# Three quarters of a conditioning product moved from VectorE to ScalarE and GpSimd

## The chip, the core and the metric

The kernel runs on one core of a Trainium2 chip. Its engines work side by side, each through its own queue in order: TensorE (PE; its weight loads are PEld) multiplies matrices, VectorE (DVE), ScalarE (ACT) and GpSimd (POOL) do elementwise work, and SyncE (SP) issues most of the DMAs that bring the weights. The metric is the device time of one execution in microseconds (us); smaller is better.

## What is computed

Two layers of a decoder trunk act on 256 tokens of 2048 features, in float32. Layer 0 has a mixer made of a gated part and a convolution, layer 1 has attention; each layer ends with a channel MLP of 8192 hidden channels. Before each of the four parts the input is normalised, scaled and shifted, and behind it the result is gated. Shift, scale and gate come from a conditioning vector `c`:

```python
c_act = jax.nn.silu(c)
for l in range(DEPTH):
    mod = c_act @ ada_w[l] + ada_b[l]
    shift1, scale1, gate1, shift2, scale2, gate2 = jnp.split(mod, 6, axis=-1)
    h = _modulate(_rms(x, norm1_g[l]), shift1, scale1)
    ...
    x = x + gate1[:, None, :] * mix
    h = _modulate(_rms(x, norm2_g[l]), shift2, scale2)
    x = x + gate2[:, None, :] * (jnp.square(jax.nn.relu(h @ mlp_w1[l])) @ mlp_w2[l])
```

`ada_w[l]` is 2048 by 12288, so the conditioning is a product of one vector with a large matrix: much weight traffic, little arithmetic for each weight. The change concerns `shift2` and `scale2` of layer 0.

## The kernel before

**Weights.** Each product of the tokens with a weight matrix runs over tiles of 512 by 512 weights (1 MiB). `wraw` (L111) issues the tile's DMA from SyncE into one of four buffers of the pool `raw`. `wtile` (L124) splits the tile into a high and a low part: ScalarE converts the tile (`wh`, L94) and VectorE subtracts that from it (`wl`, L95, both operands in SBUF). There are three buffers for `wh` and two for `wl`. A tile then feeds 24 matmuls of 128x512 (three for each of 4 feature blocks and 2 halves of the tokens, L183 to L185, or L210 to L212 in the first products of the MLP).

**Side work.** Behind each weight tile `side_work` (L135) takes steps from `ada_queue`, so many to a tile as the step's rate says. A conditioning step loads 1 MiB of `ada_w` into a `raw` buffer, too, multiplies it by values of `c` and adds it up. `ada_until` (L332) runs the steps that are left at once when their result is needed.

**The columns.** `ada_quarters` (L246) computes two columns side by side, here shift and scale of the MLP in layer 0 (columns 3 and 4). It goes by quarters of 512 features: eight steps to a quarter (four groups of inputs for each of two columns), four products to a step. A sum lies in `accq`, [128, 512] for each column, in two sets that alternate by quarter. In three quarters of the four, VectorE does product and sum in one instruction (L269), and the first product of a sum by L267. In the first quarter (`aided=1`) ScalarE makes the product (L263) into one of four places of the tile `side`, and GpSimd adds it to the sum (L265). When a sum is complete, `ada_finish_col` transposes it on TensorE (L107), reduces it on VectorE (L221) and adds the bias (L223).

**Where this lies.** `even` (L474) builds 32 such steps (L507). The eight of the first quarter are mixed with the steps of the mixer's gate row (`ada_row`, L278, which also uses ScalarE, GpSimd and `side`). The other 24 follow beside the tiles of the mixer's output product (`ab_w_out`, 16 tiles): four of them at rate `RA` (2.5 to a tile), twenty at `R1` (0.8 to a tile). The MLP then begins at L419. Its loop (L430 to L437) forces a quarter's steps (`ada_until`, L432), normalises and modulates 512 features (`norm_quarter`, L373: `xn` L354 on VectorE, transposes, `full` L380 on ScalarE, `h_h` L382 and `h_l` L383 on VectorE), and runs the three first products over the quarter before (`gemm_quarter`, L189, three tiles of `mlp_w1`).

**Other names that come up.** The convolution's taps (L542) run on VectorE and read PSUM. `layer_norm` (L603) normalises the convolution's output on VectorE and ScalarE. The gate row is spread over the partitions by two matmuls for each 512 features (L311, L312), which ScalarE copies out (L313). `residual` (L401) adds to `x` (L411, L412), and `sum_squares` (L337) squares it. `x_rstd` (L342) makes the inverse root of the norm in a chain of tiny VectorE instructions (L345 to L349, with L72 to L90). Temporary tiles of 512 columns (`junk`, `xn`, `full`, `rt` and others) share six buffers of the pool `tmp` under the tag `t512`.

**Order.** The place of an instruction in its engine's queue is set by the framework when the program is built: it follows the order of the program's text, but puts an instruction ahead where its own time model says that it is ready first. Buffers and waits come from it as well. On an engine, an instruction that waits holds up all that stand behind it.

Of the kernel before, what the change touches and what calls it, by code (L numbers as in the profile page):

```python
# [42 lines left out]
class Trunk:  # L43
    def __init__(self, ctx, tc, t):
        self.tc, self.nc, self.t = tc, tc.nc, t
        pool = lambda n, b, **k: ctx.enter_context(tc.tile_pool(name=n, bufs=b, **k))
        self.const = pool("const", 1)
        self.raw = pool("raw", 4)
        self.wh = pool("wh", 3)
        self.wl = pool("wl", 2)  # L50
        self.act = pool("act", 4)
        self.tmp = pool("tmp", 6)
        self.ext = pool("ext", 1)
        self.small = pool("small", 3)
        self.mm = pool("mm", 4, space=bass.MemoryType.PSUM)
        self.tr = pool("tr", 2, space=bass.MemoryType.PSUM)
        self.ms = pool("ms", 2, space=bass.MemoryType.PSUM)
        self.ada_queue = []
        self.ada_credit = 0.0
        self.conv_queue = []  # L60
        self.hold = False
        self.first = 0  # tiles still to be split by GpSimd
        self.conv_rate = 10
        self.conv_y = {}
        self.quarters = {}

# [1 line left out]
    def rsqrt(self, out, v):  # L68
        """out = v ** -0.5 for v > 0: a first guess from the bits, a third-order step, a Newton step."""
        nc = self.nc  # L70
        n = v.shape[-1]
        nc.vector.tensor_scalar(out.bitcast(I32), v.bitcast(I32), -0.5, float(0x5F3759DF), op0=ALU.mult, op1=ALU.add)  # L72
        pool, tag = (self.small, "nr") if n <= 16 else (self.tmp, "t512")
        a = pool.tile([P, 2, n], F32, tag=tag, name="nr")
        w, b = a[:, 0, :], a[:, 1, :]

        def square_times(f):
            if n == 1:
                nc.vector.scalar_tensor_tensor(w, out, f, out, op0=ALU.mult, op1=ALU.mult)
            else:  # L80
                nc.vector.tensor_tensor(w, out, out, op=ALU.mult)
                nc.vector.tensor_tensor(w, w, f, op=ALU.mult)

        # out <- 8/3 of its third-order step, then Newton with the 8/3 taken out again
        nc.vector.tensor_scalar(b, v, -0.5 * (3 / 8) ** 3, None, op0=ALU.mult)
        square_times(v)
        nc.vector.scalar_tensor_tensor(w, w, -10 / 3, w, op0=ALU.add, op1=ALU.mult)
        nc.vector.scalar_tensor_tensor(out, w, 5.0, out, op0=ALU.add, op1=ALU.mult)
        square_times(b)
        nc.vector.scalar_tensor_tensor(out, w, 1.5 * 3 / 8, out, op0=ALU.add, op1=ALU.mult)  # L90

    def split(self, src, hi, lo, engine=None):
        """src = hi + lo, both with the 12 significant bits that one pass of the array takes."""
        self.nc.scalar.copy(hi, src)  # L94
        (engine or self.nc.vector).tensor_tensor(lo, src, hi.bitcast(F32), op=ALU.subtract)  # L95
# [6 lines left out]
    def transpose4(self, srcs):  # L102
        """Up to four [128, n] blocks -> one PSUM bank, transposed side by side."""
        ps = self.tr.tile([P, 512], F32, tag="tr", name="trp")
        for i, s in enumerate(srcs):
            w = s.shape[-1]
            self.nc.tensor.transpose(ps[:w, i * P : i * P + s.shape[0]], s, self.ident[: s.shape[0], : s.shape[0]])  # L107
        return ps

# [14 lines left out]
    def wtile(self, w, k0, nk, n0, nw):  # L124
# [3 lines left out]
        # VectorE is busy with the norm when a phase's first tiles come: GpSimd splits those  # L128
# [6 lines left out]
    def side_work(self, size=1.0):  # L135
        """Work that is spread beside the weight tiles: conditioning and the convolution."""
# [10 lines left out]
    def gemm32(self, ps, x, w, g, n0):  # L147
        """ps += x[:, 512 features of group g] @ w[those, n0:n0+512], whole float32 passes."""
# [12 lines left out]
    def gemm(self, x, xk0, w, k0, nkb, n0, nw, skew=False):  # L161
        """[256, nw] = x[:, K] @ w[K, n0:n0+nw], as two PSUM tiles of 128 tokens; with skew the
        first half of the tokens is complete well before the second."""
# [25 lines left out]
    def gemm_quarter(self, units, x, q, paired):  # L189
        """512 features of x into each of units = (psum, w, n0, nw); with paired, the first half of  # L190
        the tokens of two units goes before their second half."""
# [23 lines left out]
    # mod = silu(c) @ ada_w + ada_b, one 1 MiB piece of ada_w to a step  # L215
    def ada_finish_col(self, out, layer, j, q, acc):
        """Feature-major column sums of acc [128, 512], plus the bias."""
# [7 lines left out]
    def ada_col(self, layer, j):  # L225
        """self.mod[layer, j] = [128, 16], feature-major."""
# [19 lines left out]
    def ada_quarters(self, layer, j0, side=None, aided=0):  # L246
        """Columns j0 and j0 + 1 side by side, complete for 512 features after every eight steps.
        The first aided quarters go by ScalarE and GpSimd, with room for products in side."""
# [3 lines left out]
        def step(q, g, i):  # L252
# [6 lines left out]
            for k in range(4):  # L259
                c = self.cT[:, 4 * g + k : 4 * g + k + 1]  # L260
                if q < aided:
                    prod = acc if g + k == 0 else side[:, D + k * 512 : D + (k + 1) * 512]
# [15 lines left out]
    def ada_row(self, layer, j, side=None):  # L278
        """self.mod[layer, j] = [128, 2048], the same in every partition. With side = [128, 4096],
        the products go to ScalarE and the sums to GpSimd."""  # L280
# [37 lines left out]
    def at_end(self, last):  # L318
        """Before the last product of a stage: no more work beside it."""
# [3 lines left out]
    def ada_more(self, rate, *lists):  # L323
        """Steps to be worked off beside the coming weight tiles, rate steps to a tile."""
# [26 lines left out]
    def norm_t(self, h, q, r):  # L351
        """Four blocks of (x * r).T in PSUM."""
# [4 lines left out]
    def norm_start(self, layer, which):  # L357
        """A function that gives 512 features' (shift, gain) columns: modulate(rms(x) * g) = x * rstd * gain + shift."""
# [14 lines left out]
    def norm_quarter(self, quarter, q, pair):  # L373
        """512 features of h.T, as (hi, lo)."""
# [10 lines left out]
    def norm_mod(self, layer, which):  # L385
        """h.T (hi, lo) of modulate(rms(x) * g, shift, scale)."""
# [6 lines left out]
    def gated(self, src, gate, h, c):  # L393
        """x[:, chunk] += gate * src, for one half"""
# [6 lines left out]
    def residual(self, ps, gate, c, last, part=None):  # L401
        """x[:, chunk] += gate * (ps + part)"""
# [16 lines left out]
    def mlp(self, layer, last):  # L419
# [8 lines left out]
        # the first three chunks take the features as the modulation completes them  # L428
# [9 lines left out]
        # sums over the blocks of hidden channels  # L438
# [35 lines left out]
    def even(self, layer):  # L474
# [14 lines left out]
        # mixer B  # L489
# [17 lines left out]
        g1, q34 = self.ada_row(layer, 2, side), self.ada_quarters(layer, 3, side, 1)  # L507
# [16 lines left out]
        def glu(j, pa, pg):  # L524
# [8 lines left out]
            def tap(b, k):  # L533
                # read from PSUM, which leaves GpSimd its port to SBUF
# [9 lines left out]
            # two sums side by side, so that no tap waits on the one before  # L544
# [11 lines left out]
        # mixer A  # L556
# [46 lines left out]
        def layer_norm():  # L603
            """LayerNorm over channels (the partition axis), swish."""
# [24 lines left out]
        # mixer A's rows of the first three chunks, then mixer B's  # L629
# [18 lines left out]
    def rms_columns(self, srcs):  # L648
        """1 / rms along the free axis of each of some [128, n], as the columns of one tile."""
# [18 lines left out]
    def low_rank(self, src, r, gcol, pair, k0, h):  # L668
        """One half's [128, 512], scaled by its rms r and by g, transposed and split."""
# [11 lines left out]
    def rope(self, out, src, tab, n):  # L681
        """Rotary pairs of [128, n, 64]; tab = [128, 128]: (C1 | C2), (-S2 | S1)."""
# [8 lines left out]
    def odd(self, layer):  # L691
# [12 lines left out]
        # columns 512:1088 = c_kv and the rotary key, as pieces of 320 and 256 columns  # L704
# [21 lines left out]
        # two heads at a time: keys, values and queries, then scores, then the output, a step apart  # L726
# [10 lines left out]
        def squares(c, s, src):  # L737
            """Sums of squares of [P, half, head, n], as row s of three."""
# [20 lines left out]
        def normalized(c):  # L759
# [8 lines left out]
            # rotary pairs of both halves  # L768
# [16 lines left out]
        def scores(c):  # L785
# [3 lines left out]
            for i in range(2):  # L789
                rows = slice(i * ROPE, (i + 1) * ROPE)  # L790
                sc = self.ms.tile([P, 512], F32, tag="ms", name="sc")
                # query block 1 sees 256 keys, query block 0 the first 128
# [18 lines left out]
        def weights_t(ss):  # L811
            out = []
            for s in ss:
                # transposed: keys 0..127 for query blocks 0 and 1, keys 128..255 for block 1
# [45 lines left out]
    def setup(self):  # L860
# [15 lines left out]
        # 128-long rows that become per-partition columns  # L876
# [43 lines left out]
    def setup_even(self):  # L920
        nc, t, c = self.nc, self.t, self.const
        # conv taps: rows (tap, block) -> columns
# [12 lines left out]
        # spatial weights, lower triangle, transposed  # L935
# [10 lines left out]
    def setup_odd(self, room):  # L946
        """Mask and rotary tables, with room [128, 768] for the raw ones."""
        nc, t = self.nc, self.t
        # causal mask: query block 1 on 256 keys, then query block 0 on 128
# [9 lines left out]
        # rotary tables of both halves with the head gains  # L959
# [39 lines left out]
def rope_table():  # L999
    """cos | sin of the rotary angles, [256, 64]: by shape alone."""  # L1000
# [23 lines left out]
```

## Time and profile before

| | |
|---|---|
| timed runs | 2189.75 us median of 3 (2189.74 to 2189.92) |
| profiled execution, first to last instruction (span) | 2185.9 us |
| around the span, against the median | 3.85 us |
| instructions | 23655 |
| weight bytes read from HBM | 564.06 MB, 259 GB/s over the span |
| GpSimd busy over the span | 146.7 us (7%) |

The profile records one execution; it gives its span, and no time of its own around it. PE, DVE, ACT and POOL in its views are the engines; "busy" is the time in which an engine had an instruction running. A row of the view of groups gives line, engine, operation, output <- inputs, the shape, how many there were, and then busy time, mean duration in ns, and the idle time in front of them with the work that ended it. A timeline row gives start, duration and so on for instructions merged where they are alike and follow one another. PEclk is the share of TensorE's clock that was granted. Where a row says "A <- B", A waited for B.

### The profile page before, as it was taken

How to read it: one execution, taken by the hardware profiler on the slowest of the kernel's cores; microseconds unless marked ns; L12 is line 12 of the kernel's file. 1: busy time of each engine (PE TensorE's matmuls, PEld its weight loads, DVE VectorE, ACT ScalarE, POOL GpSimd, SP SyncE). 2: the span in 40 equal slices, each digit the busy share in tenths (PEclk: the TensorE clock that was granted, in tenths of full speed). 3: DMA queues.
4: the chain of work that ended last, by engine and by line, in shares of the span. 5: the costliest groups of instructions: out<-in, count | busy, mean ns of one | idle time of the engine just before them, and what ended most of it. 6: DMA issues, size and time to landing. Idle time of an engine off the chain costs nothing.

```text
span 2185.9 us, 23655 instructions
## 1 busy us (share of the span) xinstructions
PE 2090.9 (96%) x9138; PEld 1635.7 (75%) x9138; DVE 1564.9 (72%) x1763; ACT 932.3 (43%) x1184; POOL 146.7 (7%) x95
## 2 busy tenths in 40 slices
PE   2889999899999999999998999989999999999999
PEld 1444458678888888888888787868888888888887
DVE  6849999888777878787767878766656545554555
ACT  2135435444444334333436776444434433433432
POOL 0038710000000000000001000010000000000000
PEclk9999999899999999999999999989999999999999
DMA  9999968899898899989755646647778556556653
GB/s 350 384 346 330 332 242 295 275 317 339 315 337 315 329 326 319 339 304 334 270 174 174 211 158 214 229 154 250 256 271 264 178 192 189 189 192 192 189 191 122
DMA packets 238620, 567.70 MB, mean 260 GB/s; under 512 B 9150, under 2 KB 17784, under 8 KB 221864
## 3 DMA queue, kind: packets, MB, share of 16 engines
q1 hardware_dynamic: 236288, 562.60, 74.3%
q10 hardware_dynamic: 1564, 2.28, 0.3%
q8 instruction: 72, 1.18, 0.2%
q0 software_dynamic: 656, 1.31, 0.2%
q14 instruction: 40, 0.33, 0.0%
HBM read 564.06 MB, written 2.10 MB: 259 GB/s over the span
## 4 chain that ended last, share of the span: by engine, by line
PE 85%; DVE 9%; DMA 5%; ACT 1%; issue 1%; SPq 0%; ACTq 0%; DVEq 0%
PE mm L183 23%; PE mm L184 23%; PE mm L185 23%; PE mm L153 4%; DMA raw<-in_ada_w 4%; PE trp L107 3%; DVE accq L269 2%; DVE cvsq L542 1%; DVE wl L95 1%; PE mm L210 1%; PE mm L211 1%; PE mm L212 1%; PE sc L797 1%; PE sc L796 1%; DMA raw<-in_mlp_w 1%
## 5 line engine op out<-in xcount | busy, mean ns | idle before, releaser
L95 DVE TENSOR_TENSOR wl<-raw,wh 128x2048 fp32r<-128x2048 f32 (+2 forms) x312 | 704.7, 2259 | 424.0 <-PE mm L184 317.9
L94 ACT CAST wh<-raw 128x2048 fp32r<-128x2048 f32 (+3 forms) x316 | 596.6, 1888 | 774.1 <-PE mm L185 515.2
L183 PE MATMUL mm<-wh,f_h 128*128 128x512 f32 x1024 | 399.6, 390 | 0.0
L185 PE MATMUL mm<-wh,f_l 128*128 128x512 f32 x1024 | 399.3, 390 | 0.0
L184 PE MATMUL mm<-wl,f_h 128*128 128x512 f32 x1024 | 398.7, 389 | 0.0
L185 PE MATMUL mm<-wh,h_l 128*128 128x512 f32 (+2 forms) x928 | 358.2, 386 | 0.0
L183 PE MATMUL mm<-wh,h_h 128*128 128x512 f32 (+2 forms) x928 | 358.2, 386 | 0.0
L184 PE MATMUL mm<-wl,h_h 128*128 128x512 f32 (+2 forms) x928 | 357.0, 385 | 0.6 <-DVE wl L95 0.6
L185 PEld LDWEIGHTS mm<-wh,f_l 128*128 128x128 f32 x1024 | 192.2, 188 | 39.8
L184 PEld LDWEIGHTS mm<-wl,f_h 128*128 128x128 f32 x1024 | 192.3, 188 | 39.6
L183 PEld LDWEIGHTS mm<-wh,f_h 128*128 128x128 f32 x1024 | 192.3, 188 | 39.2
L184 PEld LDWEIGHTS mm<-wl,h_h 128*128 128x128 f32 x928 | 175.0, 189 | 34.0 <-DVE wl L95 1.1
L185 PEld LDWEIGHTS mm<-wh,h_l 128*128 128x128 f32 x928 | 174.9, 188 | 33.4
L183 PEld LDWEIGHTS mm<-wh,h_h 128*128 128x128 f32 x928 | 175.0, 189 | 32.7
L153 PE MATMUL mm<-raw,x 128*128 128x512 f32 x448 | 195.7, 596 | 1.0 <-ACT x L500 0.6
L269 DVE SCALAR_TENSOR_TENSOR accq<-raw,cT,accq 128x512 f32<-128x512 f32 x210 | 153.7, 749 | 16.6 <-DMA raw<-in_ada_w 13.3
L153 PEld LDWEIGHTS mm<-raw,x 128*128 128x128 f32 x448 | 84.6, 191 | 104.6 <-issue 98.5
L237 DVE SCALAR_TENSOR_TENSOR acc<-raw,cT,acc 128x2048 f32<-128x2048 f32 x60 | 140.8, 2346 | 9.7 <-DMA raw<-in_ada_w 9.7
L297 DVE SCALAR_TENSOR_TENSOR acc<-raw,cT,acc 128x2048 f32<-128x2048 f32 x48 | 112.7, 2347 | 4.4 <-DMA raw<-in_ada_w 4.4
L542 DVE SCALAR_TENSOR_TENSOR cvsq<-yp,convw,cvsq 128x256 f32<-128x256 f32 x240 | 96.0, 476 | 0.0
L303 POOL TENSOR_TENSOR side<-side 128x1024 f32<-128x1024 f32 x32 | 74.8, 2361 | 19.3 <-ACT side L302 19.3
L452 ACT ACTIVATE relu<-mm 128x512 f32<-128x512 f32 x60 | 35.8, 599 | 87.7 <-PE mm L185 81.5
(270 smaller groups left out, 2246.9 us busy)
## 6 DMA issues: line engine op xcount, KB each, us to landing
raw<-in_mlp_w SPq DMA_DIRECT2D x256, 1024.0 KB, 5.6
raw<-in_ada_w SPq DMA_DIRECT2D x192, 1024.0 KB, 5.4
raw<-in_ab_w_in SPq DMA_DIRECT2D x32, 1024.0 KB, 9.7
raw<-in_ab_w_out SPq DMA_DIRECT2D x16, 1024.0 KB, 8.3
raw<-in_mla_w_out SPq DMA_DIRECT2D x16, 1024.0 KB, 4.9
raw<-in_mla_w_ukv SPq DMA_DIRECT2D x8, 1024.0 KB
raw<-in_mla_w_uq SPq DMA_DIRECT2D x8, 768.0 KB, 4.8
raw<-in_mla_w_in SPq DMA_DIRECT2D x4, 1024.0 KB, 7.2
```

What stands on the lines that cost most here:

```text
L94: self.nc.scalar.copy(hi, src)
L95: (engine or self.nc.vector).tensor_tensor(lo, src, hi.bitcast(F32), op=ALU.subtract)
L107: self.nc.tensor.transpose(ps[:w, i * P : i * P + s.shape[0]], s, self.ident[: s.shape[0], : s.shape[0]])
L153: self.nc.tensor.matmul(ps[h], x[:, 4 * g + k, h * P : (h + 1) * P], raw[:, k, :], start=g + k == 0, stop=4 * g + k == KB - 1,)
L183: nc.tensor.matmul(o, a, hi[:, i, :nw], start=first, stop=False)
L184: nc.tensor.matmul(o, a, lo[:, i, :nw], start=False, stop=False)
L185: nc.tensor.matmul(o, b, hi[:, i, :nw], start=False, stop=last)
L237: nc.vector.scalar_tensor_tensor(acc, raw, self.cT[:, kb : kb + 1], acc, op0=ALU.mult, op1=ALU.add)
L269: self.last = nc.vector.scalar_tensor_tensor(acc, raw[:, k, :], c, acc, op0=ALU.mult, op1=ALU.add).ins
L297: nc.vector.scalar_tensor_tensor(acc, raw, c, acc, op0=ALU.mult, op1=ALU.add)
L303: nc.gpsimd.tensor_tensor(acc[:, sl], acc[:, sl], prod, op=ALU.add)
L542: nc.vector.scalar_tensor_tensor(o, y, wk, o, op0=ALU.mult, op1=ALU.add)
```

## The change

The function `ada_quarters` gets a further argument `late`. From the quarter `late[0]` on, a step's products go to ScalarE and its sums to GpSimd, as in the aided quarters. The product of such a quarter is put into a buffer of the tag `t512` and not into `side`. The call for the columns 3 and 4 of layer 0 passes `late=(1,)`, that is, the second, third and fourth quarter. The other call of `ada_quarters` (columns 0 and 1 of layer 0) passes nothing and stays as it is. The rest of the diff takes comments and doc strings out. Lines behind L261 move down by five.

```diff
-    def ada_quarters(self, layer, j0, side=None, aided=0):
+    def ada_quarters(self, layer, j0, side=None, aided=0, late=None):
...
-                if q < aided:
-                    prod = acc if g + k == 0 else side[:, D + k * 512 : D + (k + 1) * 512]
+                if q < aided or (late and q >= late[0]):
+                    if g + k == 0:
+                        prod = acc
+                    elif q < aided:
+                        prod = side[:, D + k * 512 : D + (k + 1) * 512]
+                    else:
+                        prod = self.tmp.tile([P, 512], F32, tag="t512", name="prod")
                     nc.scalar.activation(prod, raw[:, k, :], AF.Copy, scale=c)
                     if g + k:
                         nc.gpsimd.tensor_tensor(acc, acc, prod, op=ALU.add)
...
-        g1, q34 = self.ada_row(layer, 2, side), self.ada_quarters(layer, 3, side, 1)
+        g1, q34 = self.ada_row(layer, 2, side), self.ada_quarters(layer, 3, side, 1, (1,))
```

## The prediction

> **What bounds the kernel now.** I read the page first, then the view of windows over the stretch that the change touches, then who TensorE waited for in it, then VectorE's groups.
>
> ```profile
> span 2185.9 us, 23655 instructions
> PE 2090.9 (96%) x9138; PEld 1635.7 (75%) x9138; DVE 1564.9 (72%) x1763; ACT 932.3 (43%) x1184; POOL 146.7 (7%) x95
> ```
>
> Over the whole kernel TensorE is the bound: 96% busy. Time can be won only where it waits or runs at a low clock. The columns' last sums run on VectorE, where these two groups stand for 283 to 458 us:
>
> ```profile
> L269 DVE SCALAR_TENSOR_TENSOR accq<-raw,cT,accq 128x512 f32<-128x512 f32 x90 | 65.6, 747 | 0.6
> L267 DVE TENSOR_SCALAR accq<-raw,cT 128x512 f32<-128x512 f32 x6 | 2.8, 479 | 0.0
> ```
>
> That is 96 instructions, 24 steps of four: all that the change moves lies in this stretch of 175 us. Its windows (busy time of each engine, then PEclk, DMA share, GB/s):
>
> ```profile
> 283.00:294.00 11.00, 11.00 (x30) 5.00 (x29) 11.00 (x25) 1.90 (x1) 0.00 (x0) 1.00 0.30 109
> 294.00:330.00 36.00, 30.81 (x132) 23.51 (x131) 33.72 (x57) 13.50 (x16) 0.00 (x0) 0.86 0.67 233
> 330.00:411.00 81.00, 81.00 (x365) 66.55 (x363) 77.26 (x93) 37.27 (x37) 0.00 (x0) 1.00 0.91 316
> 411.00:458.00 47.00, 36.79 (x158) 29.86 (x158) 41.11 (x72) 20.21 (x34) 0.00 (x0) 0.85 0.77 260
> sum 175.00, PE 159.60 PEld 124.92 DVE 163.09 ACT 72.88 POOL 0.00; mean PE 39.90 PEld 31.23 DVE 40.77 ACT 18.22 POOL 0.00
> ```
>
> Here VectorE is the fuller engine (163.1 of 175 us), ScalarE has 102 us free, and GpSimd does nothing. TensorE loses time at two places, for these reasons:
>
> ```profile
> PE trp L107 <- DVE nr L87: 8.0, 1, 8.0
> PE gps L311 <- ACT gate L313: 4.4, 1, 4.4
> PE mm L210 <- DVE h_h L382: 2.3, 1, 2.3
> ```
>
> Together 14.7 us. SyncE, too, is held up by VectorE, which keeps the raw buffers:
>
> ```profile
> SPq L118 <- DVE accq L269: 66.0, 21, 10.9
> SPq L118 <- DVE wl L95: 47.2, 15, 6.7
> ```
>
> So the stretch is bound by VectorE's queue at its ends, and by TensorE from 330 to 411 us, where it never stops.
>
> **What the change removes.** 90 x 747 ns and 6 x 479 ns leave VectorE: 68.4 us of its 163.1 us by busy time.
>
> **What it adds.** 96 products on ScalarE and 90 sums on GpSimd. The same pair ran in the first quarter (min/median/max in ns):
>
> ```profile
> L263 ACT ACTIVATE side<-raw,cT x30: 705/712/722, 149.8 to 277.6; 128x512 f32<-128x512 f32 x30
> L265 POOL TENSOR_TENSOR accq<-accq,side x30: 1262/1272/1832, 152.1 to 281.2; 128x512 f32<-128x512 f32 x30
> ```
>
> ScalarE: 96 x 0.712 = 68.4 us, beside 72.9 us that it has: 141 of 175. By busy time that is covered by its free time; the price of its order is a rival below. GpSimd: 90 x 1.272 = 114.5 us, also under 175. If nothing else were shared, the change would fit. SyncE issues the same 24 DMAs of 1 MiB at the same places of its queue; only who frees their buffers changes. Transposes, reductions and bias adds of a finished column stay.
>
> **What GpSimd and VectorE share.** The trace shows them hold each other up. Before the stretch, VectorE did tiny instructions while GpSimd added:
>
> ```profile
> 245.38 0.16 DVE L72 TENSOR_SCALAR rv<-ssv 128x16 int32<-128x16 int32 x1
> 245.46 2.33 DVE L85 TENSOR_SCALAR nr<-ssv 128x16 f32<-128x16 f32 x1
> 247.71 0.47 DVE L542 SCALAR_TENSOR_TENSOR cvsq<-yp,convw,cvsq 128x256 f32<-128x256 f32 x1
> 248.10 2.00 DVE L81 TENSOR_TENSOR nr<-rv 128x16 f32<-128x16 f32 x1
> 245.37 4.70 POOL L303 TENSOR_TENSOR side<-side 128x1024 f32<-128x1024 f32 x2 [0.33 <-ACT side L302]
> ```
>
> L85 on 16 columns took 2.33 us: it ended where the first of the two additions ended. L81 took 2.00 us, to the end of the second. The convolution's tap between them, which reads PSUM, ran its 0.47 us beside the second addition. The other way round:
>
> ```profile
> 273.83 1.48 DVE L95 TENSOR_TENSOR gl<-side,gh 128x512 fp32r<-128x512 f32 x1
> 275.63 0.67 DVE L95 TENSOR_TENSOR gl<-side,gh 128x512 fp32r<-128x512 f32 x1
> 276.62 0.68 DVE L95 TENSOR_TENSOR gl<-side,gh 128x512 fp32r<-128x512 f32 x1
> 276.59 1.83 POOL L265 TENSOR_TENSOR accq<-accq,side 128x512 f32<-128x512 f32 x1 [1.83 <-ACT side L263]
> ```
>
> The first `gl` waited for an addition to end; during the third, GpSimd's sum took 1.83 instead of 1.27 us. So an instruction of VectorE that works from SBUF and an addition of GpSimd take turns, each for its whole length. What VectorE still has of this kind in the stretch:
>
> ```profile
> L95 DVE TENSOR_TENSOR wl<-raw,wh 128x2048 fp32r<-128x2048 f32 x22 | 50.3, 2287 | 3.6 <-PE mm L211 1.6 <-ACT wh L94 1.3 <-PE mm L184 0.3
> L412 DVE TENSOR_TENSOR x<-x,rt 128x512 f32<-128x512 f32 x8 | 5.5, 688 | 0.0
> L383 DVE TENSOR_TENSOR h_l<-full,h_h 128x512 fp32r<-128x512 f32 x6 | 4.1, 685 | 0.0
> L354 DVE TENSOR_SCALAR xn<-x,r 128x512 f32<-128x512 f32 x7 | 3.4, 481 | 0.0
> L382 DVE CAST h_h<-full 128x512 fp32r<-128x512 f32 x6 | 2.5, 423 | 3.5 <-ACT full L380 3.5
> L95 DVE TENSOR_TENSOR cat_l<-cvsq,cat_h 128x1024 fp32r<-128x1024 f32 x2 | 2.4, 1220 | 0.0
> L622 DVE TENSOR_TENSOR cvsq<-cvsq,rs 128x1024 f32<-128x1024 f32 x2 | 2.4, 1220 | 0.0
> L612 DVE TENSOR_TENSOR cvsq<-cvsq,mu 128x1024 f32<-128x1024 f32 x2 | 2.4, 1222 | 0.0
> L81 DVE TENSOR_TENSOR nr<-rs 128x256 f32<-128x256 f32 x2 | 0.8, 418 | 0.0
> L85 DVE TENSOR_SCALAR nr<-var 128x256 f32<-128x256 f32 x1 | 0.3, 288 | 0.0
> ```
>
> The first eight groups are 73.0 us; from L81 to L85 stand 19 small groups on SBUF (those two are the first and the last) with 8.0 us. Sum 81.0 us. The groups that read PSUM (taps, `rt`, L596, L221) aren't counted.
>
> **The sum.** Turns taken one after the other: 114.5 + 81.0 = 195.5 us in a stretch of 175, so 20.5 us too much. VectorE idled 175 - 163.1 = 11.9 us of it, mostly waiting for ScalarE and TensorE; I take it that this stays, since those waits are of the same kind afterwards: 32.4 us. Against that stands slack at the end:
>
> ```profile
> 452.65 5.38 DVE L269 SCALAR_TENSOR_TENSOR accq<-raw,cT,accq 128x512 f32<-128x512 f32 x8
> 468.42 1.29 DVE L383 TENSOR_TENSOR h_l<-full,h_h 128x512 fp32r<-128x512 f32 x2
> 479.56 0.73 PE L210 MATMUL mm<-wh,h_h 128*128 128x512 f32 x2
> ```
>
> The last sum ended at 458.0; the features that need it were ready at 469.7, and TensorE took them at 479.6, so 9.9 us of lateness cost nothing. 32.4 - 9.9 = **+22.5 us**. The earlier waits of TensorE (14.7 us) are no further gain: whatever it wins at 300 us it would wait longer for the last sums. Behind the stretch nothing makes lost time good, since TensorE's matmuls stay the same there. On the profiled span that is 2208.4; the median stands 3.85 us above its span, so **2212 us**.
>
> Unknown are: the idle time (0 to 11.9 us), the slack (0 to 9.9), a hand-over between dependent sums (none in the 1.272), and the splits. For the hand-over:
>
> ```profile
> 251.96 5.30 POOL L265 TENSOR_TENSOR accq<-accq,side 128x512 f32<-128x512 f32 x4 [1.89 <-ACT side L263]
> ```
>
> Four in 5.30 us are 1.325 each: at most 90 x 0.053 = 4.8 us more. So from 20.5 - 9.9 = 10.6 to 32.4 + 4.8 = 37.2 us: 2200 to 2227. No row shows a 128x2048 split beside an addition; its share may be 0 to 50.3 us. I take all, being the operation of `gl` (L95, 0.67 to 1.48 us) with longer rows. The Trainium skill, "SBUF — State Buffer", section "SBUF: two separate sides", says that the pair of ports that VectorE and GpSimd share is an exclusive lock for a whole instruction, for VectorE ops with two SBUF inputs among others. By that the splits count fully and the sum stays 22.5; no trace here shows it for them.
>
> **The rivals.**
>
> *Faster: VectorE's relief wins (0.13).* If splits and sums run side by side, the shared demand is 195.5 - 50.3 = 145 us, under 175. Then VectorE's 68.4 us go, the buffers come free earlier, and the gate copy (4.4) and the norm's chain (8.0 and 2.3) are on time: -14.7 us, 2175. With the low clock gone too (36 x 0.14 + 47 x 0.15 = 12.1 us) it would be 2163 at best. For it speaks VectorE's 93%; against it every row above where both worked from SBUF. It decides if the splits hold GpSimd for less than 30 us in all (175 - 145). The Trainium skill, "Perfetto Trace Analysis", section "Optimizing Scalar/DVE Operations", says that where VectorE is saturated, moving work to ScalarE or even GpSimd may pay, and warns that the latter shares a port. The trace bears out the warning.
>
> *No change (0.07).* The lock binds half of the splits: 195.5 - 25 = 170, which just fits; TensorE's waits are replaced by as many at new places: 2190.
>
> *Much slower: ScalarE's queue blocks (0.18).* A product needs one of six `t512` buffers, and gives it back only when GpSimd has added it; `junk`, `xn`, `full` and `rt` take the same six. Behind a waiting product stand ScalarE's conversions, behind these the splits and matmuls, and behind the raw buffer SyncE's next tile:
>
> ```profile
> L94 ACT CAST wh<-raw 128x2048 fp32r<-128x2048 f32 x23 | 44.0, 1911 | 81.2 <-DMA raw<-in_ab_w_out 35.8 <-DMA raw<-in_mlp_w 14.3 <-PE mm L185 11.4
> ```
>
> Worst, sums, conversion and split of each tile come one after the other: 90/22 x 1.272 + 1.911 + 2.287 = 9.4 us, x 22 = 207, and the other 30.7 us of SBUF work of VectorE: 238 - 175 - 9.9 = +53, 2243. It decides when six products (6 x 1.27 = 7.6 us of sums) don't cover the time between two conversions.
>
> That the change does nothing is excluded: `late=(1,)` meets all of q = 1, 2, 3 of this call.
>
> **How the numbers follow.** Forecast 0.62 (2200 to 2227), blocked queue 0.18 (to 2243 and a little above), faster 0.13 (2163 to 2185), no change 0.07. About 0.2% is what a measurement of this kernel can tell from no change: 2185.4 to 2194.1. So faster 0.13, same 0.08 with the fringe of the forecast, slower 0.79. The range leaves out the faster case and the last few hundredths above: 2185 to 2245.
>
> **What would show it.** GpSimd busy 114 us or more between 283 and 490 us, many of its sums well over 1.27 us and splits over 2.29 us; the last sum at 480 to 495 instead of 458; TensorE waiting near 415 and 460 to 480 us for raw DMAs, conversions or transposes of `accq`. Wrong would be: splits that stay at 2.29 us beside sums of 1.27; last sums before 460. Products waiting on sums with conversions behind them would show the blocked queue.

## The result and the profile after

| | time, us | against before |
|---|---|---|
| before | 2189.74 median of 4 runs (2186.34 to 2189.92) | 1 |
| after | 2263.74 median of 4 runs (2261.65 to 2264.58) | 1.0337, 95% interval 1.0322 to 1.0351 |

The kernel became slower by 74.0 us. The forecast was 2212.0, with a range of 2185 to 2245: the side is right, but the loss is more than three times the 22.5 us that were worked out. The profiled execution after spans 2261.6 us. Line numbers behind L261 are higher by five than in the views of before. The head of the page after (busy time, share of the span, instructions):

```profile
span 2261.6 us, 23854 instructions
PE 2103.9 (93%) x9138; PEld 1641.5 (73%) x9138; DVE 1527.4 (68%) x1667; ACT 994.2 (44%) x1280; POOL 287.5 (13%) x185
```

TensorE does the same 9138 matmuls. Its idle time is 2261.6 - 2103.9 = 157.7 us against 2185.9 - 2090.9 = 95.0 before: 62.7 us more. Its busy time is 13.0 us longer, which is the same work at a lower granted clock. Together they are the 75.7 us between the two spans. VectorE lost 96 instructions (1763 to 1667), yet its busy time fell by only 37.5 of the 68.4 us that these stood for. Part of that is counting, since busy time counts instructions that overlap once. Added up instruction by instruction, VectorE's time fell from 1656.8 to 1606.9 us, by 49.9, where the 96 had taken 70.1 (90 x 0.747 + 6 x 0.479): some 20 us came back inside the instructions that it kept.

Windows of after, over the same stretch and up to the end of the moved sums (busy of each engine, PEclk, DMA share, GB/s):

```profile
283.00:294.00 11.00, 11.00 (x30) 5.11 (x29) 11.00 (x25) 2.49 (x2) 0.00 (x0) 1.00 0.28 104
294.00:330.00 36.00, 30.99 (x140) 23.73 (x139) 15.69 (x32) 14.29 (x21) 3.92 (x3) 0.91 0.23 71
330.00:411.00 81.00, 45.01 (x180) 35.94 (x179) 37.27 (x28) 46.05 (x59) 52.10 (x35) 0.77 0.62 215
411.00:458.00 47.00, 36.03 (x141) 28.14 (x140) 24.38 (x17) 28.54 (x38) 40.23 (x25) 0.83 0.72 246
458.00:500.00 42.00, 34.97 (x149) 27.49 (x148) 31.22 (x46) 23.95 (x38) 16.75 (x9) 0.86 0.67 226
500.00:540.00 40.00, 20.92 (x84) 16.32 (x83) 12.27 (x16) 22.79 (x35) 29.45 (x21) 0.72 0.56 187
```

No engine is full in any window from 330 us on. VectorE has 37 us of work in 81 where it had 77, and from 294 to 330 us the DMAs move 71 GB/s instead of 233. So this is not a stretch with one overloaded engine; engines wait for each other. Who waited for whom (total us, times, longest):

```profile
PE trp L107 <- POOL accq L270: 33.8, 5, 13.1
PE mm L183 <- ACT wh L94: 23.8, 1, 23.8
SPq L118 <- ACT prod L268: 92.0, 16, 23.5
POOL accq L270 <- ACT prod L268: 104.1, 9, 43.5
ACT prod L268 <- POOL accq L270: 16.1, 22, 2.2
```

TensorE's two large waits are for transposes of `accq`, whose sums GpSimd had not finished, and once for a converted weight tile. GpSimd itself stood still for 104.1 us, 43.5 of them at a stretch, because ScalarE had made no product. ScalarE in turn hardly waited for GpSimd: 22 times, never over 2.2 us. The timelines of GpSimd and then of ScalarE show the 43.5 us:

```profile
279.85 2.62 POOL L270 TENSOR_TENSOR accq<-accq,side 128x512 f32<-128x512 f32 x2
325.92 11.16 POOL L270 TENSOR_TENSOR accq<-accq,prod 128x512 f32<-128x512 f32 x8 [43.45 <-ACT prod L268]
...
503.36 28.82 POOL L270 TENSOR_TENSOR accq<-accq,prod 128x512 f32<-128x512 f32 x20 [7.13 <-ACT prod L268]
```

```profile
285.15 0.72 ACT L268 ACTIVATE accq<-raw,cT 128x512 f32<-128x512 f32 x1 [0.38 <-DMA raw<-in_ada_w]
298.90 1.90 ACT L94 CAST wh<-raw 128x2048 fp32r<-128x2048 f32 x1 [13.03 <-DMA raw<-in_ab_w_out]
...
323.04 2.19 ACT L618 ACTIVATE cvsq<-cvsq 128x1024 f32<-128x1024 f32 x2 [4.59 <-DVE cvsq L617]
325.14 4.38 ACT L268 ACTIVATE prod<-raw,cT 128x512 f32<-128x512 f32 x7
```

At 285.15 ScalarE makes the first product of the second column, which goes into `accq` itself. The other products of the same two steps need a buffer of the tag `t512`. They do not run at 286 but at 325.14, right behind the squares of `layer_norm` (L618), though ScalarE was idle for 13.03 us just before 298.90, and though their tiles were there, since the first product of each had used them. In the program's text, the users of `t512` that come before them are the gate row's `gh` and `gl` and the work tile `nr` of LayerNorm's inverse root. My reading was that the buffers are handed out in that order, so that the products were put behind work that ends 40 us later. The raw buffers stay taken for as long, and SyncE waits 23.5 us. It issues the tile that TensorE waits 23.8 us for at 328.94, and ScalarE converts that tile at 352.97 only, in its queue behind LayerNorm's swish and ten more products.

What GpSimd and VectorE then do to each other is seen in these rows: the moved sums, LayerNorm's chain on 256 columns, and one split (L95).

```profile
L270 POOL TENSOR_TENSOR accq<-accq,prod x90: 1256/1290/3357, 325.9 to 530.9; 128x512 f32<-128x512 f32 x90
```

```profile
330.38 1.39 DVE L82 TENSOR_TENSOR nr<-nr,var 128x256 f32<-128x256 f32 x1
331.80 1.37 DVE L87 SCALAR_TENSOR_TENSOR nr<-nr 128x256 f32<-128x256 f32 x1
333.20 1.37 DVE L88 SCALAR_TENSOR_TENSOR rs<-nr,rs 128x256 f32<-128x256 f32 x1
...
337.40 0.43 DVE L90 SCALAR_TENSOR_TENSOR rs<-nr,rs 128x256 f32<-128x256 f32 x1
...
416.77 3.37 DVE L95 TENSOR_TENSOR wl<-raw,wh 128x2048 fp32r<-128x2048 f32 x1
```

A step of the chain that takes 0.43 us alone (L90, just past the eight sums of 325.92) took 1.37 to 1.39 beside them. A split that takes 2.29 took 3.37, and a sum that takes 1.27 took up to 3.36, which is most of a split's length more. The last sum came at 530.9 instead of 457.3, and TensorE at the end:

```profile
513.31 0.39 PE L212 MATMUL ms<-wh,h_l 128*128 128x512 f32 x1
526.79 1.12 PE L107 MATMUL trp<-ident,accq 128*128 128x128 f32 x4 [13.10 <-POOL accq L270]
532.23 1.12 PE L107 MATMUL trp<-ident,accq 128*128 128x128 f32 x4 [4.32 <-POOL accq L270]
...
538.39 0.63 PE L212 MATMUL mm<-wh,h_l 128*128 128x512 f32 x1
...
541.30 0.39 PE L210 MATMUL mm<-wh,h_h 128*128 128x512 f32 x1
```

It stands at the transposes of the two columns for 13.10 and 4.32 us, while GpSimd works off 20 sums in one go (28.82 us, 1.44 each). After such a stop its matmuls take 0.63 us for a while and not 0.39; that is where the 13.0 us of longer busy time come from.

### The profile page after: what moved, and what is told of

Read it like the earlier page. It is cut to its first block, busy times and chain, and to the rows that moved or that the text cites. A ratio compares the mean times of both kernels' runs of the same rounds, so it can differ in the third digit from the quotient of the medians.

```text
span 2261.6 us, 23854 instructions
## 1 busy us (share of the span) xinstructions
PE 2103.9 (93%) x9138; PEld 1641.5 (73%) x9138; DVE 1527.4 (68%) x1667; ACT 994.2 (44%) x1280; POOL 287.5 (13%) x185
## 4 chain that ended last, share of the span: by engine, by line
PE 79%; DVE 8%; DMA 6%; POOL 3%; ACT 2%; issue 2%; SPq 0%; POOLq 0%; ACTq 0%; DVEq 0%
PE mm L183 21%; PE mm L185 21%; PE mm L184 21%; PE mm L153 5%; DMA raw<-in_ada_w 4%; PE trp L107 3%; POOL accq L270 3%; DMA raw<-in_mlp_w 2%; DVE cvsq L547 1%; DVE wl L95 1%; DVE accq L274 1%; PE mm L210 1%; PE mm L211 1%; PE mm L212 1%; PE sc L802 1%
## 5 line engine op out<-in xcount | busy, mean ns | idle before, releaser
L95 DVE TENSOR_TENSOR wl<-raw,wh 128x2048 fp32r<-128x2048 f32 (+2 forms) x312 | 711.2, 2280 | 436.9 <-PE mm L184 310.2
L270 POOL TENSOR_TENSOR accq<-accq,prod 128x512 f32<-128x512 f32 x90 | 140.6, 1571 | 109.1 <-ACT prod L268 104.1
L297 POOL MEMSET acc<- 128x2048 f32 x3 | 5.4, 1808 | 746.7 <-DVE mod L221 491.3
L274 DVE SCALAR_TENSOR_TENSOR accq<-raw,cT,accq 128x512 f32<-128x512 f32 x120 | 88.1, 750 | 14.8 <-DMA raw<-in_ada_w 12.1
```

What stands on the lines that cost most here:

```text
L270: nc.gpsimd.tensor_tensor(acc, acc, prod, op=ALU.add)
L274: self.last = nc.vector.scalar_tensor_tensor(acc, raw[:, k, :], c, acc, op0=ALU.mult, op1=ALU.add).ins
```

## The experiments

Two theories stood against each other. **Order**: the loss comes from products that are given their buffers late, so that GpSimd begins late and raw buffers are held. **Turns**: it comes from GpSimd's sums, which are slower than VectorE's and take turns with it, as the prediction had it.

### Buffers and sums, each undone alone

Edit for the order: LayerNorm's work tile is put into a half of `cvsq` that is not in use, so that it takes no `t512` buffer.

```diff
-    def rsqrt(self, out, v):
+    def rsqrt(self, out, v, room=None):
...
-        a = pool.tile([P, 2, n], F32, tag=tag, name="nr")
+        a = room if room is not None else pool.tile([P, 2, n], F32, tag=tag, name="nr")
...
-            self.rsqrt(rs, var)
+            self.rsqrt(rs, var, sq[:, 0:2, :])
```

Edit for the turns: the late quarters' sums go to VectorE; the products stay on ScalarE.

```diff
-                        nc.gpsimd.tensor_tensor(acc, acc, prod, op=ALU.add)
+                        (nc.gpsimd if q < aided else nc.vector).tensor_tensor(acc, acc, prod, op=ALU.add)
```

The changed kernel with the first edit:

> The changed kernel, but the two work tiles of LayerNorm's inverse root no longer come from the six shared t512 buffers (they lie in the dead half of cvsq). Late-start theory (products were held on ScalarE behind LayerNorm because the shared buffers are handed out in the order of the text, so that GpSimd's first sum came at 325.9 us): the first sum comes at 305 us or earlier, TensorE's wait of 23.8 us for a conversion goes, the time falls by about 20 to 2235-2248. Port theory (the turns of VectorE and GpSimd are the cost): the start may move, the time stays at 2260-2268.

The control, the kernel before with the first edit:

> Control: the kernel before with the same edit of LayerNorm's work tiles. Both theories: no product needs those buffers, so 2186 to 2194, no change.

The changed kernel with the second edit, and with both:

> The changed kernel, but the sums of the last three quarters are VectorE's (0.69 us each), the products stay on ScalarE in the same shared buffers. GpSimd does nothing there, so no turns. Port theory: nearly all comes back, 2185-2200. Late-start theory: products still start behind LayerNorm at about 325 us and TensorE keeps a wait of some 20 us for a conversion there; 2205-2225.

> Both edits: sums on VectorE, LayerNorm's work tiles out of the shared buffers. Late-start theory: the wait for the conversion near 330 us goes, 2185-2200, so 10 to 25 us below the run with the sums on VectorE alone. Port theory: equal to that run within 4 us.

| late sums on | `nr` in `t512` | `nr` elsewhere |
|---|---|---|
| GpSimd | 2263.7 (after) | 2239.3, ratio 1.0224 (1.0176 to 1.0273) |
| VectorE | 2217.2, 1.0123 (1.0066 to 1.0181) | 2204.2, 1.0062 (1.0043 to 1.0082) |
| control: before | 2188.4 in this series | 2189.4, 1.0004 (0.9993 to 1.0015) |

The sums in the run with `nr` elsewhere, from the tile's view:

```profile
L270 POOL TENSOR_TENSOR accq<-accq,prod x90: 1257/1290/3346, 307.5 to 509.3; 128x512 f32<-128x512 f32 x90
```

The first sum came 18.4 us earlier (307.5 for 325.9), the last 21.6 us earlier, and the time fell by 24.5 us. The same edit does nothing to the kernel before. So the place of one temporary tile in the text, far from the change, held the products back: order is real. But turns is real as well. Without GpSimd's sums the time falls by 46.6 us, or by 35.0 where the order has been eased. Neither theory alone carries the 74 us, and with both edits some 16 us are left. That run, at 2204.2, lies outside both of its forecasts (2185 to 2200, and within 4 us of 2217.2). The order is worth 24.5 us with the sums on GpSimd and 13.0 with the sums on VectorE; whether that difference is real the times do not show, since two of the four kernels have two runs each and intervals of some 11 and 13 us to either side.

### TensorE's last product moved ahead of the last sums

TensorE waits for the last quarter's transposes before it takes the third first-product of the MLP, for which the features are complete. Here the product goes first, in the changed kernel with `nr` elsewhere and, as a control, in the kernel before.

```diff
-            if q < 4:
+            late_norm = layer == 0 and q in (3,)
+            if q < 4 and not late_norm:
                 self.ada_until(lambda: self.quarters.get((layer, 3), 4) > q)
                 self.norm_quarter(quarter, q, x)
...
+            if late_norm:
+                self.ada_until(lambda: self.quarters.get((layer, 3), 4) > q)
+                self.norm_quarter(quarter, q, x)
```

> The changed kernel with LayerNorm's work tiles out of the shared buffers, and in the MLP's loop the third product (over quarter 2) now stands ahead of the last quarter's forced steps and norm. In TensorE's queue 26 and 52 of that product's matmuls now stand ahead of the last two transposes of the sums, which waited 12.9 and 4.3 us. Theory of the waiting transposes (TensorE, in order, stands behind sums that GpSimd makes too slowly): the two waits shrink by up to 52 x 0.228 = 12 us, less some 3 us of norm that is now in the open; 2227 to 2234. Theory that the end of the last sum sets the time whatever stands ahead: 2236 to 2243.

> Control: the kernel before with the same change of order in the MLP's loop alone. Its transposes waited for no sum, so there is nothing to win; the last quarter's norm, which had 9.9 us to spare, comes into the open: 2189 to 2200. A gain here would mean that the order, not GpSimd, is what the run before it shows.

Measured: 2250.6 us from two runs that lie apart (2243.6 and 2257.5; ratio 1.0291, 1.0214 to 1.0368), above both forecasts, and 2207.6 for the control (1.0095, 1.0066 to 1.0124), above its forecast too. The exchange costs the kernel before 21 us by itself. The traces show where. These are the windows from 560 us to the end: the changed kernel with `nr` elsewhere, the same with the exchange, the kernel before, and the control.

```profile
560.00:2239.00 1679.00, 1655.51 (x7657) 1368.24 (x7655) 1140.20 (x1035) 739.69 (x918) 21.02 (x11) 0.99 0.71 241
560.00:2242.00 1682.00, 1648.92 (x7614) 1360.75 (x7612) 1137.32 (x1031) 737.01 (x915) 21.03 (x11) 0.99 0.71 240
560.00:2186.00 1626.00, 1602.76 (x7422) 1324.72 (x7420) 1099.04 (x1012) 717.09 (x901) 21.00 (x11) 0.99 0.70 238
560.00:2205.00 1645.00, 1609.43 (x7427) 1327.62 (x7425) 1105.49 (x1015) 719.04 (x902) 21.02 (x11) 0.99 0.70 237
```

The control stands only five matmuls behind at 560 us (7427 to go for 7422) and then takes 19 us longer for nearly the same number. So its price does not lie at the last quarter's norm, which the forecast had in mind, but far behind it, and what causes it there no run shows. On the changed kernel the wait for sums fell from 12.9 and 4.3 us to one of 9.9. At 560 us TensorE is 43 matmuls ahead (7614 to go for 7657), some 9 us, and the run then loses some 12 us behind that point, as the control does. In these profiled executions, one of each kernel, the theory of the waiting transposes is borne out in the stretch: TensorE's wait can be filled in part. The total hides it, because the exchange costs more elsewhere.

### Fewer sums moved

With `nr` elsewhere, only the last quarter is moved (30 sums), and then only its second column (15 sums).

```diff
-        g1, q34 = self.ada_row(layer, 2, side), self.ada_quarters(layer, 3, side, 1, (1,))
+        g1, q34 = self.ada_row(layer, 2, side), self.ada_quarters(layer, 3, side, 1, (3,))
```

```diff
-                if q < aided or (late and q >= late[0]):
+                if q < aided or (late and q >= late[0] and i == 1):
```

> LayerNorm's work tiles out of the shared buffers, and only the last quarter by ScalarE and GpSimd (30 sums in place of 90); the two others stay with VectorE. Port and slow sums: the last quarter is the one that TensorE stood behind for 17 us (12.9 and 4.3), so most of its share remains; 2200 to 2215. Late-start theory: nothing is held behind LayerNorm any more, 2186 to 2194.

> As the run before it, but only the scale column of the last quarter goes to ScalarE and GpSimd (15 sums), VectorE keeps the shift column: both engines work on the same quarter. If GpSimd's pace is the cost, 15 sums of 1.34 us (20 us) fit beside VectorE's 16 products (12 us) and the rest of its work in the 54 us that the last quarter took before: 2184 to 2196. If any use of GpSimd beside the splits costs, 2196 to 2205.

Measured: 2207.2 us (1.0093, 1.0064 to 1.0122) and 2197.8 (1.0051, 1.0031 to 1.0071), against 2186.7 for the kernel before in the same series. Both lie where the theory that GpSimd's sums cost had them (2200 to 2215, 2196 to 2205). That is 20.6 us for 30 sums, 11.1 us for 15, and 50.9 us for 90 in the run with all: 0.57 to 0.74 us for each sum, somewhat more than the 0.53 by which a sum on GpSimd (1.272) is longer than the instruction of VectorE that it replaces (0.747). Neither of these parts of the change pays. The smaller one shows TensorE at the transposes. First the kernel before, then the run with 15 sums:

```profile
460.28 0.39 PE L212 MATMUL ms<-wh,h_l 128*128 128x512 f32 x1
460.51 1.03 PE L107 MATMUL trp<-ident,accq 128*128 128x128 f32 x8
```

```profile
454.67 0.39 PE L212 MATMUL ms<-wh,h_l 128*128 128x512 f32 x1
455.99 0.65 PE L107 MATMUL trp<-ident,accq 128*128 128x128 f32 x4 [0.93 <-DVE accq L274]
463.87 1.11 PE L107 MATMUL trp<-ident,accq 128*128 128x128 f32 x4 [7.23 <-POOL accq L270]
```

Before, TensorE comes from its matmuls straight to the transposes at 460.51, 2.5 us after the last sum (458.0). In the run with 15 sums the last sum ends 5.9 us later than before, at 463.9, TensorE waits 7.23 us for it, and the time grows by 11.1. The prediction had 9.9 us of lateness that cost nothing, up to the use of the features; but TensorE works in order, and the transposes stand ahead in its queue. The lateness that is free is 2.5 us.

### An early begin

If order is the products' late begin, then moving the first four late steps ahead of the gate row's finish gives their products the buffers before `gh` and `gl`, too. The four steps are then also taken at rate `R0` (1.2 to a tile) and no longer at `RA`. All three kernels below also have `nr` elsewhere.

```diff
-        mixed.append(g1[16])
+        mixed += [q34.pop(0) for _ in range(NA)] + [g1[16]]
         self.ada_more(R0, mixed)
-        self.ada_more(RA, q34[:NA])
-        self.ada_more(R1, q34[NA:])
+        self.ada_more(R1, q34)
```

With the sums on GpSimd, with the sums on VectorE, and in the kernel before:

> The changed kernel with the rsqrt tile out of the shared buffers (2239.3 us), and the first four moved steps put ahead of the gate row's finish in the program text, so that their products are given buffers before gh and gl are. If a late begin is what is left (first sum 307.5 us, GpSimd idle 22.5 us ahead of it), the first sum comes at 285 to 292 us, the last one at 490 to 498 instead of 510.6, and the time is 2215 to 2230. If GpSimd's rate near the end decides (TensorE's wait of 12.9 + 4.3 us before the last columns' transposes), the time stays at 2234 to 2242 whatever the begin.

> The same order, with products on ScalarE but the moved quarters' sums on VectorE (2204.2 us without the new order, 15 us above before). If those 15 us are the late begin (305.4 us instead of 293.9), the time falls to 2186 to 2196. If they are the price of products on ScalarE with a sum that must wait for each, it stays at 2200 to 2206.

> Control: the kernel before with the rsqrt tile out of the shared buffers and the same four steps ahead of the gate row's finish. Without a price of its own the order gives 2186 to 2194; if VectorE's sums delay gl and with it the gate, 2194 to 2205.

| | first and last sum begin, us | time, us | ratio to before | above before, us |
|---|---|---|---|---|
| sums on GpSimd | 283.4, 491.7 | 2229.15 (2225.7 to 2233.5) | 1.0185 (1.0165 to 1.0205) | 40.4 |
| sums on VectorE | 280.8, 462.8 | 2200.98 (2197.6 to 2201.3) | 1.0051 (1.0036 to 1.0066) | 12.2 |
| before, same order | 280.5, 456.3 | 2194.18 (2189.8 to 2196.0) | 1.0024 (1.0014 to 1.0033) | 5.4 |

The first of them, by the view of the tile, by the waits, and by the groups on GpSimd and VectorE:

```profile
L270 POOL TENSOR_TENSOR accq<-accq,prod x90: 1259/1295/3244, 283.4 to 491.7; 128x512 f32<-128x512 f32 x90
```

```profile
PE trp L107 <- POOL accq L270: 15.1, 4, 5.2
POOL accq L270 <- ACT prod L268: 53.9, 9, 27.0
```

```profile
L270 POOL TENSOR_TENSOR accq<-accq,prod 128x512 f32<-128x512 f32 x90 | 150.4, 1678 | 59.1 <-ACT prod L268 53.9
```

```profile
L95 DVE TENSOR_TENSOR wl<-raw,wh 128x2048 fp32r<-128x2048 f32 x26 | 69.6, 2678 | 18.9 <-ACT wh L94 6.9 <-PE mm L211 6.7 <-PE mm L184 3.3
```

The begin came where it was expected to (283.4; 285 to 292 had been said), the last sum in the forecast's interval of 480 to 495, and the time at the upper end of 2215 to 2230. Some 24 us of earlier begin were worth 17.6 us at the end and 10.1 us of time. Even so the kernel stands 40.4 us above before, with sums of 1.678 us in the mean and 53.9 us in which GpSimd waits for products. With the sums on VectorE the time is 2201.0, just inside the second case (2200 to 2206): a first sum at 280.8 instead of 305.4 was worth 3 us, so the late begin is not what was left there. The control, at 2194.2, lies on the border of its two cases; the interval of its ratio excludes no change, so the new order has a small price of its own.

The traces show that this price lies elsewhere. The 1800th matmul starts at 578.6 us in the kernel before, at 653.3 in the changed kernel, and at 616.2, 585.5 and 575.6 in the three kernels of the table. At that point, behind the stretch, the first two are 37.6 and 6.9 us late and the control is 3.0 us early. Each of the three loses another 6 to 9 us further on, the control too; the cause stays open.

Undone one after the other, the parts give the 74.0 us in this order: the products' order 33.6 (74.0 - 40.4), sums on GpSimd instead of VectorE 28.2 (40.4 - 12.2), the product on ScalarE and a separate sum in place of one instruction 6.8 (12.2 - 5.4), and 5.4 for the order that served to undo the first part. The first three differences are uncertain by 4 to 6 us, the last by 2, and undone in another order the shares may differ. By the starts of the 1800th matmul the same four steps are 37.1, 30.7, 9.9 and -3.0 us, of the 74.7 by which the changed kernel is late there.

### Turns alone

So far GpSimd's sums were both slow and needed. Here the kernel before keeps all its sums on VectorE, and GpSimd makes 36 additions that nothing needs, beside 18 of the 24 late steps. They go to the half of `accq` that is not in use.

```diff
+            if idle and q >= aided and g:
+                other = box["acc"][:, (q + 1) % 2, i, :]
+                for k in range(2):
+                    nc.gpsimd.tensor_tensor(other, other, raw[:, k, :], op=ALU.add)
```

> The kernel before, all its sums on VectorE, and beside 18 of the 24 late steps two additions on GpSimd that nothing needs (36 x 1.272 = 45.8 us), into the half of accq that is not in use. If additions and VectorE's work from SBUF take turns, VectorE's 163.1 us become up to 209 in a stretch of 175: +20 to +36 us, 2210 to 2226, with splits and sums of 128x512 lengthened by up to 1.3 us. If they run side by side, 2186 to 2194, splits at 2.29 and sums at 0.75 us.

Measured: 2217.0 us (2215.3 to 2219.4), ratio 1.0130 (1.0113 to 1.0146): 28.2 us for 45.8 us of additions. The groups of VectorE from 283 to 490 us, before and then with the spare additions:

```profile
L269 DVE SCALAR_TENSOR_TENSOR accq<-raw,cT,accq 128x512 f32<-128x512 f32 x90 | 65.6, 747 | 0.6
L542 DVE SCALAR_TENSOR_TENSOR cvsq<-yp,convw,cvsq 128x256 f32<-128x256 f32 x23 | 9.1, 469 | 0.0
L412 DVE TENSOR_TENSOR x<-x,rt 128x512 f32<-128x512 f32 x8 | 5.5, 688 | 0.0
L411 DVE TENSOR_TENSOR rt<-mm,gate 128x512 f32<-128x512 f32 x6 | 4.1, 686 | 0.0
L382 DVE CAST h_h<-full 128x512 fp32r<-128x512 f32 x8 | 3.4, 423 | 3.7 <-ACT full L380 3.7
```

```profile
L269 DVE SCALAR_TENSOR_TENSOR accq<-raw,cT,accq 128x512 f32<-128x512 f32 x90 | 85.8, 972 | 0.6
L416 DVE TENSOR_TENSOR x<-x,rt 128x512 f32<-128x512 f32 x8 | 7.7, 957 | 0.0
L386 DVE CAST h_h<-full 128x512 fp32r<-128x512 f32 x6 | 5.8, 965 | 2.1 <-ACT full L384 2.1
L546 DVE SCALAR_TENSOR_TENSOR cvsq<-yp,convw,cvsq 128x256 f32<-128x256 f32 x23 | 9.1, 473 | 0.0
L415 DVE TENSOR_TENSOR rt<-mm,gate 128x512 f32<-128x512 f32 x6 | 4.1, 681 | 0.0
```

VectorE's sums grew by 20.2 us in all, from 0.747 to 0.972 in the mean. The splits hardly grew (2.33 us in the mean for 2.29): there it was the additions that waited. The instructions that read PSUM (the taps, `rt`) kept their 0.47 and 0.68 us. Where they meet, the rows show whole lengths, here VectorE's and then GpSimd's:

```profile
392.51 4.49 DVE L95 TENSOR_TENSOR wl<-raw,wh 128x2048 fp32r<-128x2048 f32 x2
396.91 1.78 DVE L269 SCALAR_TENSOR_TENSOR accq<-raw,cT,accq 128x512 f32<-128x512 f32 x1
```

```profile
393.37 6.48 POOL L273 TENSOR_TENSOR accq<-accq,raw 128x512 f32<-128x512 f32 x2 [6.37 <-DMA raw<-in_ada_w]
```

Two splits ran undisturbed (4.49), and GpSimd's two additions beside them took 6.48 us instead of 2.54. In the trace the first of them took 4.8 us, past the end of both splits; the sum behind the splits waited about 1 us for its end. GpSimd does not release the raw buffers late in this run: between 283 and 520 us no wait of SyncE or of any other engine ended on it. So the turns cost time by themselves, with no result that anything waits for and no product on ScalarE. The Trainium skill, "SBUF — State Buffer", section "SBUF: two separate sides", calls the shared pair of ports a lock for the whole instruction; these rows and the splits of 3.37 us in the changed kernel agree, for splits too, for which the trace of before had no row.

## Why the prediction was right on the side and wrong in size

- **Removed, 68.4 us from VectorE**: right as work (96 instructions less), but some 20 us of it returned as waiting inside others.
- **ScalarE's 68.4 us, "covered by its free time"**: this is the step that failed first. By busy time it was free. The products' place in its queue was not: the first came at 325.14 instead of about 286. Easing the order gave 24.5 us, and 33.6 with the early begin. The sum of 114.5 + 81.0 in 175 us silently let GpSimd begin where VectorE had begun (294) and never stand still; it began at 325.9 and stood 104.1 us waiting for products.
- **GpSimd's 90 x 1.272 = 114.5 us**: the instructions took 140.6 us by the page's group of L270. The difference is turns: the median is 1.290, the longest 3.357.
- **Turns for a whole length, splits counted fully**: right, and shown by the spare additions (28.2 us) and by the lengths above.
- **The slack of 9.9 us**: wrong, 2.5 us at the transposes, which stand ahead of the use in TensorE's queue. Without it the forecast's own sum would have been 32.4 or, with the true slack, 29.9. With the early begin the run stands 40.4 us above before, 35.0 above its control. Its profile, of the slowest of three runs, has TensorE busy for 2106.6 us instead of 2090.9, so 15.7 us of that execution's loss are a lower clock. The sum had no term for that. That the sum comes near is no proof of each term: in that run GpSimd still waited 53.9 us, which the forecast had at nothing.
- **The rival of a blocked queue** had the right engine and the wrong mechanism. It let products wait for buffers that GpSimd holds, with conversions behind them. That wait was 16.1 us in all, and never over 2.2. What held the products was the order in which buffers are given out, before any sum ran, as the two edits of that order show: the first sum came at 325.9, then 307.5, then 283.4. Conversions did stand behind products in ScalarE's queue, as at 352.97, but those ten products themselves had waited for GpSimd only 0.38 us. The time also lies 20 us above the 2243 of this rival's worst case.
- **Faster and no change** fell with the split: it does hold GpSimd, and GpSimd holds it.

Not settled is the rest of 6.8 us (9.9 at the 1800th matmul) with sums on VectorE and the early order. Two instructions in place of one, with a wait between, may be the cause, but no run takes that wait away. The kernel before remains the fastest: no version run here beats it.

## What to carry to other kernels

When work goes to an engine that has free time, look up where the new instructions will stand in that engine's queue, and which buffers they draw from a shared pool: a temporary tile that is asked for earlier in the text can hold back work that was ready 40 us before. Free time of GpSimd beside a VectorE that works from SBUF isn't free; here 45.8 us of additions that nothing needed cost 28.2 us. Measure slack at the first instruction of the consumer's queue that waits for the result, here the transposes and not the product that uses the features. A control tells that an edit has a price of its own, but not where; the start of the same matmul in both traces does.

## What the hardware showed that was not expected

Not only instructions with two operands in SBUF were held: `h_h`, a conversion of one operand from SBUF, went from 0.423 to 0.965 us in the mean beside the spare additions. And TensorE's stops cost more than their length: after waits of 13.10 and 4.32 us a matmul took 0.63 us at 538.39 and was back at 0.39 by 541.30 (starts 0.43 us apart, then 0.23); over the kernel, 62.7 us of further idle time brought 13.0 us of longer busy time. The Trainium skill, "TensorE: Matmul & The Clock Gate", section "What's actually happening", has the clock halved after an idle window of about 3.4 us and full again after as long a busy one. The waits above are longer than that and the slower matmuls agree with it; the prediction had no such term for its waits.
